# A diffusion block on one core: late modulation by PE, filter products in pairs of row halves, filter spectra from high and low parts

## The chip, the cores and the metric

The kernel runs on one core of a Trainium2 chip. The metric is the device time of one execution in microseconds; lower is better. The engines are TensorE (PE in the profile; PEld is its weight load), VectorE (DVE), ScalarE (ACT), GpSimd (POOL) and SyncE (SP). Each engine runs its own queue of instructions in order and waits for the others through semaphores. SP's queue and POOL's queue also issue the DMA transfers of this kernel.

## The reference

One layer of a transformer-like block on 1024 tokens of width 1024 with a prefix of 256 context tokens. All data are float32. What the change touches is the modulation and the filters:

```python
mod = jax.nn.silu(c) @ w_ada[i] + b_ada[i]            # (1, 6 * 1024)
mod_c = jax.nn.silu(c_ctx) @ w_ada[i] + b_ada[i]
sh1, sc1, g1, sh2, sc2, g2 = jnp.split(mod[:, None, :], N_MOD, axis=-1)
h = modulate(rmsnorm(x, norm1_g[i]), sh1, sc1)        # h * (1 + scale) + shift
q, k, v, hv, hx1, hx2, gna, ghy = jnp.split(h @ w_in[i], IN_SPLITS, axis=-1)
y_na = neighbourhood_attention(...)                   # 8 heads of 64, window 8 x 16, and all context keys
y_hy = hyena_mixer(hv, hx1, hx2, *hy_params)          # 2 long convolutions over 512 channels
x = x + g1 * gated_merge(gna, ghy, y_na, y_hy, w_na_o[i], w_hy_o[i], w_out[i])
h2 = modulate(rmsnorm(x, norm2_g[i]), sh2, sc2)
x = x + g2 * swiglu(h2, ffn_w1[i], ffn_w3[i], ffn_w2[i])   # hidden width 2816
return rmsnorm(x, final_g)

def hyena_filters(L, ...):                            # inside hyena_mixer
    hid = jnp.sin(fr * (hid @ w2 + b2))               # (1024, 64)
    h = (hid @ w3).reshape(L, 2, HY_ORDER, HY_WIDTH)  # forward and backward filter of 2 orders, 512 channels
    return h * decay[:, None, None, :]

def long_conv_bidir(u, h_fwd, h_bwd, bias):           # z = gate * this, twice
    K = jnp.fft.rfft(k2, n=2 * L, axis=0)             # k2: both filters, joined
    U = jnp.fft.rfft(u, n=2 * L, axis=1)
    y = jnp.fft.irfft(U * K[None], n=2 * L, axis=1)[:, :L]
    return y + u * bias
```

## The kernel before, in words

A tile framework schedules the program: it gives each engine a fixed order of instructions, and it allocates tiles from pools in rings. A tile's tag names its ring, and `bufs` says how many buffers the ring has; a tile that gets a buffer again waits until its former user is done. Instructions passed to `keep_in_program_order` stay in the order of the code; others the scheduler may move.

Large products are made in float32r, with each operand split into a high and a low part (`split`: ACT casts to the high part, DVE subtracts it from the source for the low part). `gemm` then adds three products, low times high, high times low and high times high (the matmuls of L194). A few products use plain float32, where the trace shows two records for each matmul (x2).

By time the stages are:

- 0 to 73 us: modulation for the first norm, the norm, and the small network that makes `hid` for the filters.
- 73 to 338 us, the filter stage. The input projection is made in 40 chunks (`proj`, tiles `in_ps` and `ctx_ps`, weights `wr` by SP, split into `wh`, `wl`). Between its pieces a side generator (`side`) makes the filters and their spectra (`filters`) and, merged with these, sums for the modulation's late parts (`ada_sums`). `_merged` interleaves generators by their yields' values against the totals that are given (`SIDE` against 39 for the projection, 97 and 39 inside the side).
- 338 to 650 us: the long convolutions (`conv`) as the side, with the projection going on.
- 650 to 805 us: neighbourhood attention with the rest of the projection.
- 805 to 950 us: the rest of attention, merged with hyena's output product (`hyena_out`, tiles `yhraw`, `hy_ps`) and with `ada_late`. This interleaving is written in the loop of `run` over `attention`.
- 950 to 1752 us: the merge, the second norm and the feed-forward network.

`filters` has four groups, one for each half of the channels and each order. A group makes 8 banks of filter products (`filt_ps`, L349), each from two float32 matmuls with 64 rows: index `j` picks rows 0 to 63 or 64 to 127 of the array. DVE multiplies a bank by `dec`, which SP loads (256 KB each, ring of 2), into `fv` (L353). Radix steps on DVE follow (`fx`, `x`, `b`), then eight DFTs of 128 points on 2 x 256 columns (`parts` makes the operand `a` on DVE and loads a matrix `matf` for two DFTs; `dft` makes three float32 matmuls, L425 to L427, into `dft_ps`). ACT copies the spectrum to `ks`, and SP stores it. The same `forward` and `dft` also serve the convolutions. The banks `f` of PSUM that `filt_ps` and `dft_ps` use are a ring of five.

`ada_sums` (L843) makes, for each of the four late parts of the modulation, the sum over 8 row blocks of `w_ada` times silu(c): SP loads `wal` (512 KB, ring of 1), and DVE does `aacc` += `wal` times a column of `cs` (L853). What is left is a sum over the 128 partitions; `aacc` is stored by POOL. `ada_late` (L857) loads the stored sums (`acc`, L868) and sums over partitions by matmuls with ones (`al_ps`, L877 to columns for the second norm's shift and scale, L890 to full tiles for the gates `g1` and `g2`).

Of the kernel before, what the change touches and what calls it, by code (L numbers as in the profile page):

```python
# [10 lines left out]
F32 = mybir.dt.float32  # L11
# [7 lines left out]
P = 128  # L19
D = 1024  # L20
# [3 lines left out]
SIDE = 460  # L24
# [18 lines left out]
def _constants():  # L43
# [15 lines left out]
    out["dft_f"], out["dft_i"] = fwd, inv  # L59

# [98 lines left out]
class Block:  # L159
# [176 lines left out]
    def filters(self, pool, psf, hid, w3):  # L336

        nc, a = self.nc, self.a
        for hf in range(2):
            for o in range(2):  # L340
                v = [pool.tile([P, 4, 2, 256], F32, tag="v8", name="fv") for _ in range(2)]
                c0 = o * 512 + hf * 256
                for n2 in range(0, 8, 2):
                    for j in range(2):
                        dec = pool.tile([P, 512], F32, tag="dec", name="dec", bufs=2)
                        nc.sync.dma_start(dec, a["decay"][hf, n2 // 2, j])
                        ps = psf.tile([P, 512], F32, tag="f", name="filt_ps")
                        for n in range(2):
                            nc.tensor.matmul(ps[:, n * 256:(n + 1) * 256],  # L349
                                             hid[64 * j:64 * j + 64, (n2 + n) * P:(n2 + n + 1) * P],  # L350
                                             w3[64 * j:64 * j + 64, c0:c0 + 256], start=True, stop=True)
                        i = n2 % 4
                        nc.vector.tensor_tensor(v[n2 // 4][:, i:i + 2, j, :], ps.rearrange("p (n c) -> p n c", n=2),  # L353
                                                dec.rearrange("p (n c) -> p n c", n=2), op=ALU.mult)
                    yield 1.3
# [11 lines left out]
                parts, spectra = self.forward(pool, psf, v[1], x)  # L367
# [10 lines left out]
    def forward(self, pool, psf, wp, wm):  # L378
# [19 lines left out]
        def parts():  # L398
# [10 lines left out]
            m = pool.tile([P, 2, 3, P], F32, tag="mat", name="matf")  # L409
            nc.sync.dma_start(m, self.a["dft_f"][ci])  # L410
            for j in range(2):
                av = pool.tile([P, 2, 256], F32, tag="a", name="a")
# [3 lines left out]
        def spectra():  # L416
            for _ in range(2):
                yield self.dft(psf, *queue.pop(0))
# [3 lines left out]
    def dft(self, psf, m, v):  # L422
# [4 lines left out]
        nc.tensor.matmul(ps[:, 256:512], m[:, 2], v[:, 0], start=False, stop=True)  # L427
        return ps
# [414 lines left out]
    def ada_sums(self, pool):  # L843

        nc, a = self.nc, self.a
        for part in range(2, 6):
            acc = pool.tile([P, D], F32, tag="aacc", name="aacc", bufs=1)
            nc.vector.memset(acc, 0.0)
            nc.sync.dma_start(acc[0:1, :], a["b_ada"][0:1, part * D:(part + 1) * D])
            for k in range(8):  # L850
                w = pool.tile([P, D], F32, tag="wal", name="wal", bufs=1)
                nc.sync.dma_start(w, a["w_ada"][k, :, part * D:(part + 1) * D])
                nc.vector.scalar_tensor_tensor(acc, w, self.cs[:, 2 * k:2 * k + 1], acc, op0=ALU.mult, op1=ALU.add)  # L853
                yield 1.2
            nc.gpsimd.dma_start(self.accd[part], acc)

    def ada_late(self, pool, psf, gates):  # L857

        nc = self.nc
        pin = self.tc.keep_in_program_order  # L860
        ones = pool.tile([P, P], F32, name="ones")
        nc.vector.memset(ones, 1.0)

        def load(part):
            accs = []
            for h in range(2):
                accs.append(pool.tile([P, 512], F32, tag="acc", name="acc", bufs=4))
                nc.sync.dma_start(accs[h], self.accd[part][:, h * 512:(h + 1) * 512])  # L868
            return accs

        queue = [(part, load(part)) for part in (3, 4)]
        yield
        ps = psf.tile([P, 512], F32, tag="f", name="al_ps")
        for n, (part, accs) in enumerate(queue):
            for k in range(8):
                at = 16 * n + 2 * k
                pin(nc.tensor.matmul(ps[:, at:at + 2], accs[k // 4][:, (k % 4) * P:(k % 4 + 1) * P], ones[:, 0:2],  # L877
                                     start=True, stop=True))
            src = ps[:, 16 * n:16 * n + 16].rearrange("p (k t) -> p k t", t=2)[:, :, 0]
            if part == 3:  # L880
                nc.vector.tensor_copy(self.mod2[:, 1, :], src)
            else:
                nc.vector.scalar_tensor_tensor(self.mod2[:, 0, :], src, 1.0, self.ng[:, 1, :],
                                               op0=ALU.add, op1=ALU.mult)
        queue = [(part, load(part)) for part in (2, 5)]
        yield
        for part, accs in queue:
            for h in range(2):
                ps = psf.tile([P, 512], F32, tag="f", name="al_ps")
                pin(nc.tensor.matmul(ps, ones, accs[h], start=True, stop=True))  # L890
# [556 lines left out]
```

## Time and profile before

| what | value |
|---|---|
| time, median of 3 runs | 1752.66 us (1752.51 to 1756.64) |
| the profiled execution's own time | 1753.88 us |
| its span, first to last instruction | 1752.0 us |
| mean granted PE clock | 0.978 |
| DMA moved | 285.36 MB, 163 GB/s |

The profile shows one execution. Busy times are of one engine over the span or over a named stretch. A row of a group gives the line, the engine, the operation with its output and inputs, the count, then busy time and mean duration, then the idle time of that engine just before these instructions with what ended it. In the timeline the columns are start, duration, engine, line, operation, count; in brackets stands the idle time before and what ended it. A PE record's duration includes its passage through the array, so that the distance between two starts is what one costs in a dense run.

### The profile page before, as it was taken

What the parts mean: (1) busy time and instruction counts of PE and PEld (TensorE: products, weight loads), DVE (VectorE), ACT (ScalarE), POOL (GpSimd) and SP (SyncE); (2) the same over time, 40 slices, a digit from 0 to 9 for tenths busy, and PEclk for the clock granted to TensorE, in tenths of its full rate; (3) what the DMA queues carried; (4) which work ended last, traced back from release to release, by engine and by line L of the source; (5) the groups of instructions that cost most, each with busy time, mean ns of one, the idle gap of its engine ahead of it and who ended that gap; (6) DMA issues with size and microseconds to landing.
All of it is one profiled execution on the core that took longest, in us unless ns stands there. A gap on an engine that the chain in (4) does not pass through costs nothing.

```text
span 1752.0 us, 22510 instructions
## 1 busy us (share of the span) xinstructions
PE 1674.1 (96%) x8128; PEld 1325.2 (76%) x8128; DVE 1227.8 (70%) x2039; ACT 663.5 (38%) x1147; POOL 143.2 (8%) x250
## 2 busy tenths in 40 slices
PE   6989898999999998999999999899999999999997
PEld 2777676777777777887777788688888888877886
DVE  5576576799887865656865867867755656479567
ACT  4611222313121213546654215733343333344555
POOL 0000110001000004011200000000100000100000
PEclk8999999999999999999999999999999999999999
DMA  8266766655464528436647424333422332295344
GB/s 352 103 220 207 224 214 201 213 162 174 145 209 148 180 73 246 129 115 192 204 157 250 158 68 144 126 120 115 150 91 91 104 107 97 102 368 186 101 120 151
DMA packets 111469, 285.36 MB, mean 163 GB/s; under 512 B 14707, under 2 KB 23543, under 8 KB 109053
## 3 DMA queue, kind: packets, MB, share of 16 engines
q1 hardware_dynamic: 91888, 221.32, 38.3%
q0 software_dynamic: 18816, 62.14, 10.4%
q8 instruction: 65, 1.06, 0.3%
q10 hardware_dynamic: 653, 0.44, 0.1%
q14 instruction: 47, 0.39, 0.1%
HBM read 213.86 MB, written 69.99 MB: 162 GB/s over the span
## 4 chain that ended last, share of the span: by engine, by line
PE 50%; issue 29%; DMA 8%; DVE 7%; ACT 3%; POOL 3%; SPq 0%; POOLq 0%; ACTq 0%; DVEq 0%
PE in_ps L194 19%; PE dx_ps L1315 5%; PE dft_ps L425 4%; PE out_ps L1089 4%; PE dz_ps L1315 3%; PE dft_ps L426 2%; PE dft_ps L427 2%; PE x_ps L1151 2%; DMA ar<-g 1%; POOL g L1263 1%; PE dy_ps L1315 1%; PE pt_ps L761 1%; PE na_ps L194 1%; PE pt_ps L775 1%; POOL g L1257 1%
## 5 line engine op out<-in xcount | busy, mean ns | idle before, releaser
L194 PE MATMUL in_ps<-hTh,wl 128*128 128x512 f32 x640 | 259.6, 406 | 5.2 <-ACT proj L596 5.2
L194 PE MATMUL in_ps<-hTl,wh 128*128 128x512 f32 x640 | 253.3, 396 | 0.0
L194 PE MATMUL in_ps<-hTh,wh 128*128 128x512 f32 x640 | 253.2, 396 | 0.0
L194 PEld LDWEIGHTS in_ps<-hTh,wl 128*128 128x128 f32 x640 | 121.8, 190 | 33.0 <-ACT proj L596 5.8
L194 PEld LDWEIGHTS in_ps<-hTh,wh 128*128 128x128 f32 x640 | 122.1, 191 | 26.6 <-issue 0.7
L194 PEld LDWEIGHTS in_ps<-hTl,wh 128*128 128x128 f32 x640 | 122.3, 191 | 25.8 <-issue 1.3
L175 DVE TENSOR_TENSOR ol<-ws,oh 128x512 fp32r<-128x512 f32 x88 | 60.5, 689 | 54.8 <-ACT oh L174 54.7
L174 ACT CAST wh<-wr 128x1024 fp32r<-128x1024 f32 x40 | 42.0, 1049 | 127.4 <-PE in_ps L194 103.5
L175 DVE TENSOR_TENSOR ol<-ar,oh 128x512 fp32r<-128x512 f32 x77 | 52.9, 688 | 49.0 <-ACT oh L174 49.0
L175 DVE TENSOR_TENSOR wl<-wr,wh 128x1024 fp32r<-128x1024 f32 x40 | 48.8, 1221 | 53.3 <-ACT wh L174 53.2
L174 ACT CAST oh<-ar 128x512 fp32r<-128x512 f32 x77 | 47.9, 622 | 84.3 <-PE dx_ps L1315 33.4
L425 PE MATMUL dft_ps<-a,matf 128*128 128x512 f32 x128 | 68.9, 621 | 10.0 <-issue 5.5
L174 ACT CAST oh<-ws 128x512 fp32r<-128x512 f32 x88 | 54.7, 622 | 53.8 <-PE x_ps L1151 23.7
L749 DVE CUSTOM_DVE_ANT_0 pe<-s_ps,bias 128x640 f32<-128x640 f32 x64 | 50.1, 819 | 30.4 <-PE s_ps L744 30.4
L853 DVE SCALAR_TENSOR_TENSOR aacc<-wal,cs,aacc 128x1024 f32<-128x1024 f32 x32 | 41.0, 1282 | 43.3 <-DMA wal<-in_w_ada 43.1
L1315 PE MATMUL dx_ps<-oh,ol 128*128 128x512 f32 x176 | 67.1, 391 | 3.6 <-DVE ol L175 3.6
L1315 PE MATMUL dx_ps<-ol,oh 128*128 128x512 f32 x176 | 68.7, 390 | 1.7 <-DVE ol L175 1.7
L750 ACT ACTIVATE pe<-pe,mx 128x640 f32<-128x640 f32 x64 | 52.6, 822 | 44.0 <-DVE mx L749 43.9
L1315 PE MATMUL dx_ps<-oh 128*128 128x512 f32 x176 | 68.5, 389 | 0.0
L175 DVE TENSOR_TENSOR ol<-wr,oh 128x512 fp32r<-128x512 f32 x70 | 48.0, 689 | 27.0 <-ACT oh L174 26.9
L174 ACT CAST oh<-wr 128x512 fp32r<-128x512 f32 x70 | 43.1, 621 | 54.6 <-PE y_ps L1151 18.2
L1091 DVE TENSOR_TENSOR x<-x,out_ps 128x512 f32<-128x512 f32 x64 | 43.5, 685 | 22.3 <-PE out_ps L1089 22.2
(392 smaller groups left out, 4236.9 us busy)
## 6 DMA issues: line engine op xcount, KB each, us to landing
wr<-in_w SPq DMA_DIRECT2D x50, 512.0 KB, 3.4
wr<-in_w_in SPq DMA_DIRECT2D x40, 512.0 KB, 4.5
ar<-g SPq DMA_DIRECT2D x77, 256.0 KB, 2.8
wal<-in_w_ada SPq DMA_DIRECT2D x32, 512.0 KB, 4.0
g<-t POOLq DMA_DIRECT2D x49, 256.0 KB, 2.8
matf<-in_dft_f SPq DMA_DIRECT2D x32, 384.0 KB, 4.9
bias<-in_rpb SPq DMA_DIRECT2D x64, 192.0 KB, 2.8
w<-in_w SPq DMA_DIRECT2D x44, 256.0 KB, 5.4
```

Source lines behind the costliest of these rows:

```text
L174: self.nc.scalar.copy(hi, src)
L175: self.nc.vector.tensor_sub(lo, src, hi.bitcast(F32))
L194: mm = nc.tensor.matmul(ps, ww[:, k * P:(k + 1) * P], xx[:, k, pos:pos + width], start=(i == 0), stop=(i == n - 1))
L425: nc.tensor.matmul(ps, m[:, 0], v.rearrange("p a b -> p (a b)"), start=True, stop=False)
L426: nc.tensor.matmul(ps[:, 0:256], m[:, 1], v[:, 1], start=False, stop=False)
L427: nc.tensor.matmul(ps[:, 256:512], m[:, 2], v[:, 0], start=False, stop=True)
L749: nc.vector.tensor_tensor_reduce(pe, ps[:, 256:896], bt, -1.0, 3e38, ALU.add, ALU.min, mx[:, 0:1])
L750: nc.scalar.activation(pe, pe, AF.Exp, bias=mx[:, 0:1], scale=-1.0, accum_out=mx[:, 1:2])
L853: nc.vector.scalar_tensor_tensor(acc, w, self.cs[:, 2 * k:2 * k + 1], acc, op0=ALU.mult, op1=ALU.add)
L1089: nc.tensor.matmul(ps, gg[x][:, tk], ww[y][:, sl], start=(i == 0), stop=(i == n - 1))
L1091: nc.vector.tensor_add(x1[:, sl], x1[:, sl], ps)
L1315: nc.tensor.matmul(ps[j], x[u][:, j * P:(j + 1) * P], w[v], start=(start and i == 0 and c == 0), stop=(stop and i == N - 1 and k == len(re ...
```

## The change

1. `ada_sums` and `ada_late` are replaced by `ada_rows`. PE multiplies the `cs` columns (32 columns) by `wal`: four float32 matmuls of 256 columns for a row block, each into another group of 32 columns of the array (L892 after), summed over eight row blocks in one bank (`ar_ps`), which holds two parts. The ring of `wal` has two buffers. DVE adds the bias row; POOL stores four short rows for each part in `modd`; four transposes turn the second norm's shift and scale into columns. The gates are later loaded from `modd` by broadcast.
2. The filter products of two banks are made in the order n, then j, kept in program order, so that neighbours use different row halves.
3. The filters' spectra use `dft_parted`: the operand is split into `ah` and `a`, the matrix `matr` holds high and low parts, and nine float32r matmuls take the place of three float32 ones. A matrix (384 KB) serves one DFT, and POOL's queue loads it. The convolutions' DFTs stay as they are.

```diff
-SIDE = 460
+SIDE = 447
...
+    out["dft_r"] = np.ascontiguousarray(np.stack([hi, fwd - hi], 3).transpose(0, 2, 1, 3, 4, 5))
...
+                    dec, ps = [], []
                     for j in range(2):
-                        dec = pool.tile([P, 512], F32, tag="dec", name="dec", bufs=2)
...
+                        dec.append(pool.tile([P, 512], F32, tag="dec", name="dec", bufs=2))
+                        nc.sync.dma_start(dec[j], a["decay"][hf, n2 // 2, j])
+                        ps.append(psf.tile([P, 512], F32, tag="f", name="filt_ps"))
+                    for n in range(2):
+                        for j in range(2):
+                            mm = nc.tensor.matmul(ps[j][:, n * 256:(n + 1) * 256],
+                                                  hid[64 * j:64 * j + 64, (n2 + n) * P:(n2 + n + 1) * P],
+                                                  w3[64 * j:64 * j + 64, c0:c0 + 256], start=True, stop=True)
+                            if n + j:
+                                self.tc.keep_in_program_order(mm)
...
-                            k = pool.tile([P, 512], F32, tag="ks", name="ks", bufs=3)
+                            k = pool.tile([P, 512], F32, tag="ks", name="ks", bufs=2)
...
+                if parted:
+                    m = pool.tile([P, 2, 3, P], F32R, tag="mat", name="matr")
+                    nc.gpsimd.dma_start(m, self.a["dft_r"][ci, j])
+                    av, ah = (pool.tile([P, 2, 256], F32R, tag=t, name=t) for t in ("a", "ah"))
+                    raw = pool.tile([P, 2, 256], F32, tag="ar", name="ar", bufs=1)
+                    nc.vector.scalar_tensor_tensor(raw, x, -g if j else g, b[:, 0], op0=ALU.mult, op1=ALU.add)
+                    self.split(ah, av, raw)
+                    queue.append((m, (ah, av)))
+                    continue
...
+    def dft_parted(self, psf, m, v):
+        ps = psf.tile([P, 512], F32, tag="f", name="dft_ps")
+        order = ((1, 0), (0, 1), (0, 0))
+        for i, (x, y) in enumerate(order):
+            nc.tensor.matmul(ps, m[:, x, 0], v[y].rearrange("p a b -> p (a b)"), start=(i == 0), stop=False)
+        for x, y in order:
+            nc.tensor.matmul(ps[:, 0:256], m[:, x, 1], v[y][:, 1], start=False, stop=False)
+        for i, (x, y) in enumerate(order):
+            nc.tensor.matmul(ps[:, 256:512], m[:, x, 2], v[y][:, 0], start=False, stop=(i == 2))
...
-    def ada_sums(self, pool):
-    def ada_late(self, pool, psf, gates):
+    def ada_rows(self, pool, psf):
...
+        for pair in ((3, 4), (2, 5)):
+            r = pool.tile([P, 512], F32, tag="arow", name="arow", bufs=1)
+            nc.gpsimd.memset(r, 0.0)
...
+                    nc.gpsimd.dma_start(r[32 * j:32 * j + 1, 256 * n:256 * n + 256], a["b_ada"][0:1, at:at + 256])
+            ps = psf.tile([P, 512], F32, tag="f", name="ar_ps")
+            for n, part in enumerate(pair):
+                for k in range(8):
+                    w = pool.tile([P, D], F32, tag="wal", name="wal", bufs=2)
+                    nc.sync.dma_start(w, a["w_ada"][k, :, part * D:(part + 1) * D])
+                    for j in range(4):
+                        nc.tensor.matmul(ps[32 * j:32 * j + 32, 256 * n:256 * n + 256], self.cs[:, 2 * k:2 * k + 32],
+                                         w[:, 256 * j:256 * j + 256], start=(k == 0), stop=(k == 7),
+                                         tile_position=(0, 32 * j))
+                    yield 0.8
+            nc.vector.tensor_add(r, ps, r)
...
+                    nc.gpsimd.dma_start(self.modd[part][0:1, 256 * j:256 * j + 256],
+                                        r[32 * j:32 * j + 1, 256 * n:256 * n + 256])
...
-                        fgen = self.filters(_Bufs(fp, t4=1, mat=2, a=2, b=4), psf, hid, w3)
-                        yield from _merged((fgen, 97), (self.ada_sums(fp), 39))
+                        fgen = self.filters(_Bufs(fp, t4=1, mat=2, a=2, ah=2, b=4), psf, hid, w3)
+                        yield from _merged((fgen, 97), (self.ada_rows(fp, psf), 26))
...
-                g1, g2 = (yp.tile([P, D], F32, name=n) for n in ("g1", "g2"))
+                nc.gpsimd.dma_start(g1, self.modd[2].broadcast_to((P, D)))
...
-                nc.sync.dma_start(self.gate2, g2)
...
-        for t, src in ((fg, a["fg"].broadcast_to((P, D))), (g2, self.gate2)):
+        for t, src in ((fg, a["fg"].broadcast_to((P, D))), (g2, self.modd[5].broadcast_to((P, D)))):
```

PE's queue at the end of a group's DFTs and the first products of the next group, before:

```order
L427 MATMUL dft_ps_1197<-a_1188,matf_1184 128x256
L349 MATMUL filt_ps_1208<-fw3_273,hid_272 128x256 x2
L349 MATMUL filt_ps_1214<-fw3_273,hid_272 128x256 x2
L349 MATMUL filt_ps_1227<-fw3_273,hid_272 128x256 x2
L349 MATMUL filt_ps_1233<-fw3_273,hid_272 128x256 x2
L349 MATMUL filt_ps_1239<-fw3_273,hid_272 128x256 x2
```

Each bank is written by two matmuls in a row, and eight banks follow one another without other work between. After, the same place, with the last rows of the group's products:

```order
L459 MATMUL dft_ps_1310<-ah_1292,matr_1289 128x256
L353 MATMUL filt_ps_1327<-fw3_272,hid_271 128x256
L353 MATMUL filt_ps_1330<-fw3_272,hid_271 128x256
...
L196 MATMUL in_ps_1399<-hTh_251,wl_1167 128x512
L353 MATMUL filt_ps_1375<-fw3_272,hid_271 128x256
L196 MATMUL in_ps_1399<-hTl_252,wh_1166 128x512
L196 MATMUL in_ps_1399<-hTh_251,wh_1166 128x512
L353 MATMUL filt_ps_1378<-fw3_272,hid_271 128x256
```

Two banks now alternate, and three matmuls of the projection stand inside the fourth pair of the group.

PE's queue at a DFT of the first group after the change, where a row block of the modulation comes between:

```order
L459 MATMUL dft_ps_1049<-ah_936,matr_933 128x256
L892 MATMUL ar_ps_843<-wal_1158,cs_240 32x256 x2
L455 MATMUL dft_ps_1062<-ah_944,matr_941 128x512
L892 MATMUL ar_ps_843<-wal_1158,cs_240 32x256 x2
L196 MATMUL in_ps_1197<-hTh_251,wh_951 128x512
...
L455 MATMUL dft_ps_1062<-a_943,matr_941 128x512
L455 MATMUL dft_ps_1062<-ah_944,matr_941 128x512
L457 MATMUL dft_ps_1062<-ah_944,matr_941 128x256
```

Matmuls of three kinds alternate there; before, three `dft_ps` matmuls stand together at such a place, with only the projection around them.

SP's queue where hyena's output begins, before (`yh` is the stored output of the convolutions, `bias` are the attention's tables):

```order
L868 DMA acc_6341<-acc3_213 128x512
L868 DMA acc_6343<-acc3_213 128x512
L868 DMA acc_6345<-acc4_214 128x512
L868 DMA acc_6347<-acc4_214 128x512
L826 DMA yhraw_6351<-yh0_100 128x512
L826 DMA yhraw_6355<-yh0_100 128x512
L868 DMA acc_6521<-acc2_212 128x512
L868 DMA acc_6523<-acc2_212 128x512
L868 DMA acc_6525<-acc5_215 128x512
L826 DMA yhraw_6359<-yh1_101 128x512
```

And after:

```order
L723 DMA kcraw_7319<-kc3_115 128x256
L858 DMA yhraw_6816<-yh0_100 128x512
L858 DMA yhraw_6820<-yh0_100 128x512
L182 DMA wfr_7086<-in_why 128x512
L763 DMA bias0_5498<-in_rpb 128x384
L763 DMA bias1_5499<-in_rpb 128x384
L858 DMA yhraw_6824<-yh1_101 128x512
L858 DMA yhraw_6828<-yh1_101 128x512
```

The eight `acc` loads are gone, and the loads of `yhraw` stand ahead of the weights `wfr` and the tables.

More of the change, by code (lines that the diff above doesn't have):

```diff
@@ L839, in hyena_out @@
                 yield
-    def ada_sums(self, pool):
+    def ada_rows(self, pool, psf):
         nc, a = self.nc, self.a
[L846 to L855, printed above, removed]
@@ L857, in ada_late @@
-    def ada_late(self, pool, psf, gates):
[L859 to L883, printed above, removed]
-                                               op0=ALU.add, op1=ALU.mult)
[L885 to L890, printed above, removed]
-                nc.scalar.copy(gates[part][:, h * 512:(h + 1) * 512], ps)
-                yield
@@ L915, in run @@
             self.hyd = [dt(f"hyo{c}", (P, T)) for c in range(8)]
-            self.accd = {j: dt(f"acc{j}", (P, D)) for j in range(2, 6)}
+            self.modd = {j: dt(f"mod{j}", (1, D)) for j in range(2, 6)}
             self.gd = [dt(f"gate{c}", (P, T)) for c in range(16)]
@@ L993, in run @@
                             next(hyena, None)
-                        elif n != 0:
-                            next(late, None)
-                    for gen in (late, hyena):
-                        for _ in gen:
-                            pass
+                    for _ in hyena:
+                        pass
                     att.close()
-                nc.sync.dma_start(self.gate2, g2)
                 psf = E3(tc.tile_pool(name="psf3", bufs=8, space=PSUM))
```

43 lines of the change are left out of this document (26 added, 17 removed).

## Prediction

> **What bounds the kernel now.** I read the page first, then the busy time by stage, then the groups and the DMA issues of the stage that the change touches, and last the timeline at the places where instructions move. The busy table and the chain of the page:
>
> ```profile
> PE 1674.1 (96%) x8128; PEld 1325.2 (76%) x8128; DVE 1227.8 (70%) x2039; ACT 663.5 (38%) x1147; POOL 143.2 (8%) x250
> PE 50%; issue 29%; DMA 8%; DVE 7%; ACT 3%; POOL 3%; SPq 0%; POOLq 0%; ACTq 0%; DVEq 0%
> ```
>
> TensorE (PE) is busy for 96% of the span, and half of the chain is PE. So a microsecond of PE work counts almost fully, and what a faster VectorE (DVE) is worth must be read stage by stage. The change touches the filter stage (73 to 338 us) and the first part of the attention beside hyena's output (805 to 836 us). Columns below: stretch, length, busy time of PE, PEld, DVE, ACT and POOL, the granted PE clock, DMA share, GB/s.
>
> ```profile
> 73.00:139.00 66.00, 60.93 (x286) 46.77 (x284) 45.62 (x58) 14.25 (x26) 3.80 (x7) 0.97 0.67 220
> 139.00:148.00 9.00, 6.76 (x35) 4.73 (x34) 5.10 (x7) 0.59 (x1) 0.00 (x0) 0.83 0.93 321
> 148.00:210.00 62.00, 57.81 (x264) 44.88 (x265) 37.98 (x44) 14.19 (x25) 5.02 (x7) 0.92 0.59 186
> 210.00:220.00 10.00, 7.35 (x42) 5.20 (x41) 5.47 (x7) 0.59 (x1) 0.00 (x0) 1.00 0.79 247
> 220.00:274.00 54.00, 53.36 (x240) 41.20 (x238) 42.54 (x55) 15.46 (x25) 6.56 (x9) 0.97 0.62 201
> 274.00:290.00 16.00, 11.33 (x49) 8.04 (x48) 6.94 (x9) 0.59 (x1) 0.00 (x0) 0.79 0.84 289
> 290.00:338.00 48.00, 48.00 (x211) 37.03 (x211) 39.99 (x55) 15.41 (x23) 5.06 (x7) 1.00 0.51 162
> ...
> 805.00:836.00 31.00, 26.23 (x216) 21.31 (x214) 22.27 (x53) 21.62 (x42) 0.56 (x1) 0.86 0.73 230
> ```
>
> In the filter stage PE idles 5.1 + 2.2 + 4.2 + 2.7 + 0.6 + 4.7 = 19.5 us. The missing clock (length times one minus the clock: 2.0 + 1.5 + 5.0 + 1.6 + 3.4) is worth 13.5 us more: 33 us lost in 265. The three short stretches are where a group of filters begins; there the DMA share is highest (0.79 to 0.93). From 805 to 836 us 4.8 us are idle and 4.3 lost to the clock. What the losses of the filter stage hang on, DVE's groups and then PE's:
>
> ```profile
> L853 DVE SCALAR_TENSOR_TENSOR aacc<-wal,cs,aacc 128x1024 f32<-128x1024 f32 x32 | 41.0, 1282 | 43.3 <-DMA wal<-in_w_ada 43.1 <-DMA aacc<-in_b_ada 0.2
> L353 DVE TENSOR_TENSOR fv<-filt_ps,dec 128x512 f32<-128x512 f32 x32 | 21.1, 683 | 10.2 <-DMA dec<-in_decay 6.7 <-PE filt_ps L349 3.5
> ...
> L848 DVE MEMSET aacc<- 128x1024 f32 x4 | 3.6, 912 | 12.7 <-DMA acc<-aacc 9.2 <-DMA matf<-in_dft_f 3.2 <-DVE hcTl L175 0.3
> ```
> ```profile
> L425 PE MATMUL dft_ps<-a,matf 128*128 128x512 f32 x64 | 36.1, 647 | 9.4 <-issue 5.5 <-DVE a L413 3.9
> L349 PE MATMUL filt_ps<-fw,hid 64*128 64x256 f32 x128 | 25.6, 414 | 10.1 <-DVE fv L353 10.1
> ```
>
> PE's 19.5 us stand in front of two kinds of matmul: the filter products, which need a free bank (the multiply by `dec` frees it), and the first DFT of a group. DVE itself stood 43 us before `aacc`, waiting for `wal`, and its queue runs in order, so part of PE's wait may be `aacc`'s doing; 6.7 us are `dec`'s own landing.
>
> **The DFTs.** A float32 DFT is three matmuls. From the first to the first of the next:
>
> ```profile
> 124.59 1.02 PE L425 MATMUL dft_ps<-a,matf 128*128 128x512 f32 x2
> ...
> 126.31 1.02 PE L425 MATMUL dft_ps<-a,matf 128*128 128x512 f32 x2
> ```
>
> That is 1.72 us. The new one is nine float32r matmuls, three of 512 columns and six of 256. The projection runs such matmuls back to back at full clock:
>
> ```profile
> 87.97 0.39 PE L194 MATMUL in_ps<-hTh,wl 128*128 128x512 f32 x1
> 88.20 0.39 PE L194 MATMUL in_ps<-hTl,wh 128*128 128x512 f32 x1
> ...
> 98.21 0.28 PE L194 MATMUL ctx_ps<-hcTl,wh 128*128 128x256 f32 x1
> 98.33 0.28 PE L194 MATMUL ctx_ps<-hcTh,wh 128*128 128x256 f32 x1
> ```
>
> So 0.23 and 0.12 us each: 3 x 0.228 + 6 x 0.119 = 1.40. 32 DFTs x 0.32 us = **10.2 us less** PE work. The parts cost a cast on ACT and a subtraction on DVE, 32 of each, like these:
>
> ```profile
> L175 DVE TENSOR_TENSOR ol<-ar,oh 128x512 fp32r<-128x512 f32 x77 | 52.9, 688 | 49.0 <-ACT oh L174 49.0
> ...
> L174 ACT CAST oh<-ar 128x512 fp32r<-128x512 f32 x77 | 47.9, 622 | 84.3 <-PE dx_ps L1315 33.4
> ```
>
> ACT gains 20 us where it has 60 busy of 265, so nothing. DVE gains 22 us and loses `aacc` with its clearing, 41.0 + 3.6: 23 us lighter. The single buffer of `ar` makes DVE wait for ACT once a DFT; the projection's work covers that except at a group's first DFT.
>
> **The filter products.** In the order n, then j, neighbours use different row halves. Of before:
>
> ```profile
> 89.11 0.39 PE L194 MATMUL in_ps<-hTh,wh 128*128 128x512 f32 x1
> 89.42 1.13 PE L349 MATMUL filt_ps<-fw,hid 64*128 64x256 f32 x4
> 90.48 0.50 PE L194 MATMUL in_ps<-hTh,wl 128*128 128x512 f32 x1
> ...
> 139.28 4.26 PE L349 MATMUL filt_ps<-fw,hid 64*128 64x256 f32 x28
> ```
>
> 28 records took 4.26 us. One after the other, at 0.215 us for 256 columns (1.72 / 8: a DFT is 2048 column passes), they would take 6.0; in perfect pairs 3.0. They overlap half already. Perfect pairs save at most 128 x (0.152 - 0.107) = 5.7 us, but behind them stands the wait for banks. I take **-2** (0 to -6).
>
> **The modulation's sums on PE.** 128 matmuls of 256 columns, four per weight row into four column groups. Before has the same form with 512 columns:
>
> ```profile
> 26.66 1.06 PE L288 MATMUL ada_ps<-wada,cs 128*32 128x512 f32 x8
> ```
>
> Eight records, that is four matmuls of two passes, took 1.06 us with their latency (0.2): 0.86, the time of one. So four with 256 columns are 0.43 us, and 32 rows 13.8. They are not in one piece: the order has about 26 visits between other matmuls. The steps around L349 at 89.42 show what a change of kind costs: 0.31 us instead of 0.23 into it and 0.34 instead of 0.23 out of it, 0.18 in all. 26 x 0.18 = 4.7. Together **+18.4** (13.8 if the changes overlap; 32 x 1.72 = 55 if the columns ran one after the other), and the four transposes +0.6.
>
> The Trainium skill ("TensorEngine Tiling (Array Packing)", Key Properties) says that the array drains when its tiling changes. The 0.18 us are what these rows show of it.
>
> **The late part.** Its matmuls and the loads ahead of hyena's go:
>
> ```profile
> L890 PE MATMUL al_ps<-acc,ones 128*128 128x512 f32 x8 | 4.5, 645 | 0.0
> L877 PE MATMUL al_ps<-ones,acc 128*128 128x2 f32 x32 | 4.1, 258 | 0.3 <-DVE mod L881 0.3
> ```
> ```profile
> 833.86 0.50 PE L194 MATMUL hy_ps<-yhh,wfl 128*128 128x512 f32 x1 [2.38 <-ACT yhh L174]
> ```
> ```profile
> 810.74 0.91 SPq L826 DMA_DIRECT2D yhraw<-yh  x2
> 814.55 2.52 SPq L868 DMA_DIRECT2D acc<-acc  x3
> ```
>
> 4.5 + 4.1 us of PE go, at a clock of 0.86. Hyena's inputs `yhraw` move up past the eight `acc` loads on SP, so the 2.4 us wait at 833.86 may go. But the attention's steps here wait for softmax, and PE with less to fill in may idle instead. **-9** (-4, half of the matmuls; -13, matmuls and 4.4 of the 9.1 us lost). The gates' broadcasts (POOL, SP) replace the `acc` and `gate2` transfers and land long before their use: 0.
>
> **The waits of the filter stage.** This is the largest uncertainty. What feeds it:
>
> ```profile
> wal<-in_w_ada SPq DMA_DIRECT2D x32, 512.0 KB, 4.0
> dec<-in_decay SPq DMA_DIRECT2D x32, 256.0 KB, 4.2
> ...
> matf<-in_dft_f SPq DMA_DIRECT2D x16, 384.0 KB, 4.9
> acc<-aacc POOLq DMA_DIRECT2D x4, 512.0 KB, 5.6
> ```
> ```profile
> 134.09 0.54 POOL L855 DMA_DIRECT2D acc<-aacc  x1 [17.07 <-DVE x L408]
> ```
>
> A matrix of 384 KB now serves one DFT instead of two, through the same two buffers, on POOL's queue; POOL's stores in this queue (`qk`, `kc`, `vtok`) come between. By the rows a matrix takes 4.9 us to land; where the order puts DFTs densest, at some 7 places, the DFT that needs the freed buffer follows after 3.5 to 4.2 us of PE work (their matmuls by the pitches above): with POOL's 0.5 for the issue 1.2 to 1.9 us each, 11 us of waits (2 if it lands in 4, as a `wal` does; 25 if it takes 6.3, above the 5.6 of the POOL row). PE now frees `wal` (two buffers, 4.0 us, against 3.0 to 3.5 us of work between rows in the densest places, again some 7): 6 (2 to 14). SP's queue stands behind each `wal` that waits, with `dec` and the spectra's stores. The first DFT of each group keeps 6, `dec` 3, half clock 5. That makes 31 in place of 33: **-2** (-15 to +20, from these bounds).
>
> What a wait does beyond its length:
>
> ```profile
> 218.33 1.13 PE L349 MATMUL filt_ps<-fw,hid 64*128 64x256 f32 x4 [2.65 <-DVE fv L353]
> ...
> 219.96 0.63 PE L194 MATMUL in_ps<-hTh,wl 128*128 128x512 f32 x1
> ```
>
> After a wait of 2.65 us the same matmul takes 0.63 instead of 0.39 us. The Trainium skill ("TensorE: Matmul & The Clock Gate", Why this matters for your kernels) would have only gaps above some 3.4 us cost clock; here the shorter one did, so I let waits of 2 us count for clock as well.
>
> **The sum.** -10.2 - 2 + 18.4 + 0.6 - 9 - 2 = -4.2 us. The profiled execution took 1753.9 us (span 1752.0 and 1.9 around it), 1.2 above the median 1752.66: 1752.7 - 4.2 = 1748.5, said as **1748 us**. Less than 0.3% (5.3 us) can't be told from no change.
>
> **The rivals.**
>
> *The waits go with `aacc`.* For it: 43.1 us of DVE's waiting stood before `aacc`, in the queue that frees banks and makes `a`. Against it: 6.7 us of `fv`'s wait is `dec`'s own, and the DMA share there stays. If 14 of the 31 us that I let stand go too: 1734 (1726 to 1741).
>
> The Trainium skill ("DMA: Bandwidth & Descriptors", Anatomy of one DMA, SWDGE (gpsimd) path) fits 2.0 us plus bytes at 436 GB/s for such a transfer: an estimate of 2.9 us for a matrix, by which the matrix waits vanish and the sum is about -15. No load of this size from POOL's queue stands in before.
>
> *The matrices stop PE.* The other side, by one mechanism: two buffers with one DFT each. Each microsecond that a matrix takes beyond 4.9 adds some 10 us (7 places, and the half clock behind). It decides from about 5.8 us, where the sum is +5; at 6.3 it is +10: 1762 (1754 to 1775). For it: the DMA share of 0.79 to 0.93 where groups begin, and 16 more matrices of 384 KB. Against: 0.6 elsewhere.
>
> *The columns don't overlap* beside single visits, at 1.7 us a row instead of 0.43: +40, 1780 and more. The row at 26.66 speaks against it.
>
> *The late part brings nothing*, because softmax sets the pace there: 1757 (1752 to 1760).
>
> **How the numbers follow.** The sum as worked (1742 to 1754): 0.45, of which 0.20 is faster by over 0.3% and 0.25 within. Waits go: 0.22, faster. Matrices stop PE: 0.20, 0.06 within and 0.14 slower. Columns one after the other: 0.05, slower. Late part brings nothing: 0.08, 0.06 within and 0.02 slower. Faster 0.42, within 0.3% 0.37, slower 0.21. The range 1731 to 1766 takes the first case and that of the late part whole, 0.14 of the 0.22 where waits go and 0.13 of the 0.20 where matrices stop PE, 0.80 in all; the likeliest's own is 1742 to 1754.
>
> **What would show it.** After: nine float32r matmuls per DFT in 1.4 us; four `ar_ps` matmuls of a visit in about 0.6 us; `matr`'s median landing near 4.9; the first `dft_ps` matmuls' idle time near 11 us by `matr`, not by DVE; the stretch before conv ending within 5 us of 338 + 5 (the sum without the late part); hyena's first matmuls without the wait for `yhh`. The prediction is wrong if the loss of the filter stage leaves 20 to 45 us, or if a visit costs over 0.9 us.

## Result and profile after

The changed kernel takes 1774.51 us (median; 1770.77 to 1774.82) against 1752.59 of the kernel before: a ratio of 1.0122, with a 95% interval of 1.0100 to 1.0143. It is slower by some 22 us, above the predicted range. The profiled execution has a span of 1772.7 us.

Busy table and chain of the page, to be read against those of before:

```profile
PE 1674.5 (94%) x8444; PEld 1325.3 (75%) x8444; DVE 1208.2 (68%) x2036; ACT 678.4 (38%) x1175; POOL 175.8 (10%) x313
PE 58%; DVE 5%; issue 5%; DMA 5%; ACT 2%; POOL 0%; SPq 0%; DVEq 0%; POOLq 0%; ACTq 0%
```

PE is as busy as before (1674.5 against 1674.1 us), and the span is 20.7 us longer. So in sum the loss is idle PE. The filter stage by stretches (the columns of the prediction; the stage now ends later, so a last stretch is added):

```profile
73.00:139.00 66.00, 58.29 (x363) 42.85 (x362) 41.40 (x59) 18.61 (x33) 11.93 (x23) 1.00 0.74 237
139.00:148.00 9.00, 7.37 (x38) 5.79 (x40) 1.55 (x3) 1.17 (x2) 1.05 (x2) 0.81 1.00 310
148.00:210.00 62.00, 53.63 (x289) 40.84 (x288) 34.39 (x46) 14.82 (x26) 10.01 (x18) 0.92 0.59 186
210.00:220.00 10.00, 10.00 (x50) 8.12 (x50) 1.61 (x3) 1.17 (x2) 0.54 (x1) 1.00 0.62 186
220.00:274.00 54.00, 49.13 (x311) 37.09 (x310) 35.51 (x50) 16.40 (x29) 12.08 (x20) 1.00 0.61 187
274.00:290.00 16.00, 11.04 (x51) 8.05 (x52) 2.41 (x4) 3.54 (x8) 3.41 (x6) 0.75 0.83 275
290.00:338.00 48.00, 46.68 (x256) 35.23 (x253) 37.36 (x55) 12.21 (x20) 4.93 (x8) 0.98 0.56 173
338.00:360.00 22.00, 18.84 (x103) 14.83 (x102) 9.50 (x15) 8.42 (x14) 7.13 (x13) 1.00 0.68 199
```

PE idles 32.0 us in these 287 us; the kernel before idles 20.5 in the same ones. In the three short stretches the idle time fell from 9.6 to 6.6 us, in the others (73 to 139, 148 to 210, 220 to 274, 290 to 338 us) it rose from 9.9 to 22.3. The missing clock, by the same rows, is 11.6 us, against 13.5 before. What PE waits for, in us, times, longest (73 to 365 us):

```profile
PE dft_ps L455 <- DMA matr<-in_dft_r: 20.7, 12, 3.9
PE ar_ps L892 <- DMA wal<-in_w_ada: 5.1, 5, 2.4
PE filt_ps L353 <- DVE fv L360: 3.0, 1, 3.0
PE ar_ps L892 <- DMA wr<-in_w_in: 1.9, 1, 1.9
PE dft_ps L455 <- ACT ah L176: 0.4, 1, 0.4
```

The waits for `fv` fell from 10.1 to 3.0 us, and those for `a` and issue are gone. In their place stand the matrices with 20.7 us and the weight rows with 7.0. One cycle of it, in PE's timeline, POOL's, and PE's again:

```profile
119.67 0.28 PE L459 MATMUL dft_ps<-ah,matr 128*128 128x256 f32 x1
```
```profile
120.25 0.53 POOL L424 DMA_DIRECT2D matr<-in_dft_r  x1 [3.31 <-PE dft_ps L459]
```
```profile
123.15 0.40 PE L196 MATMUL in_ps<-hTh,wh 128*128 128x512 f32 x1
125.85 0.47 PE L455 MATMUL dft_ps<-ah,matr 128*128 128x512 f32 x1 [2.30 <-DMA matr<-in_dft_r]
126.16 0.40 PE L196 MATMUL in_ps<-hTh,wl 128*128 128x512 f32 x1
126.39 0.39 PE L196 MATMUL in_ps<-hTl,wh 128*128 128x512 f32 x1
```

The DFT that holds the buffer ends at 119.95 (119.67 + 0.28). POOL has waited for it 3.31 us and starts the next matrix at 120.25. The DFT that needs it starts 5.60 us later, at 125.85, with PE idle for the last 2.30. At the 12 waits the time from POOL's issue to the DFT is 4.2 to 7.3 us, 5.6 on average, and the landing alone, counted from the start of the issue, 5.5. POOL issued within 0.8 us of the buffer's release at 11 of them. At one it issued 4.3 us late, since a store ahead in its queue (`vctok`) waited for ACT; that wait of 1.9 us hangs on the queue, not on the ring alone. The transfers' medians in the stage (SP's and POOL's queue):

```profile
wal<-in_w_ada SPq DMA_DIRECT2D x32, 512.0 KB, 4.9
matr<-in_dft_r POOLq DMA_DIRECT2D x32, 384.0 KB, 4.7
```

For a balance I give each instant from 73 us to the last matmul of the projection to the PE instruction that then runs (from its start to the next start or its own end), with the rest as idle. Smaller kinds are left out, so the rows shown don't add up to the last one (us):

| | before | after | dft_only | rows_only | no_parted | hi_ring4 | mat4 | mat4_half |
|---|---|---|---|---|---|---|---|---|
| filters' DFTs | 58.9 | 51.7 | 49.0 | 55.6 | 55.7 | 50.3 | 54.2 | 51.3 |
| filter products | 24.7 | 24.1 | 26.3 | 23.7 | 21.7 | 22.6 | 27.4 | 26.1 |
| `ar_ps` | 0 | 17.9 | 0 | 17.5 | 17.5 | 18.5 | 18.3 | 30.1 |
| `in_ps` (1824 each) | 435.2 | 437.7 | 436.6 | 432.6 | 430.5 | 431.9 | 438.4 | 437.3 |
| idle | 26.1 | 39.9 | 39.5 | 17.1 | 20.8 | 25.9 | 37.5 | 24.9 |
| whole stretch | 731.6 | 758.6 | 738.1 | 737.6 | 734.8 | 738.3 | 764.5 | 759.2 |

Each column is one execution. It lies up to 4.4 us from its kernel's median (`mat4_half` 4.4 and `rows_only` 3.8 above, `no_parted` 3.3 below), so differences of a few us between columns need not be the kernels'.

Up to there the change loses 27.0 us. From there to hyena's last matmul it gains 3.8 (145.0 to 141.2), and behind that 2.5 (802.4 to 799.9), against a span 20.7 longer.

### The profile page after: what moved, and what is told of

Same layout as the page of the kernel before. It is cut to its first block, busy times and chain, and to the rows that moved or that the text cites. A ratio compares the mean times of both kernels' runs of the same rounds, so it can differ in the third digit from the quotient of the medians.

```text
span 1772.7 us, 23235 instructions
## 1 busy us (share of the span) xinstructions
PE 1674.5 (94%) x8444; PEld 1325.3 (75%) x8444; DVE 1208.2 (68%) x2036; ACT 678.4 (38%) x1175; POOL 175.8 (10%) x313
## 4 chain that ended last, share of the span: by engine, by line
PE 58%; DVE 5%; issue 5%; DMA 5%; ACT 2%; POOL 0%; SPq 0%; DVEq 0%; POOLq 0%; ACTq 0%
PE x_ps L1160 13%; PE in_ps L196 12%; PE z_ps L1160 7%; PE dx_ps L1324 6%; PE out_ps L1098 3%; PE dz_ps L1324 3%; PE y_ps L1160 2%; PE dft_ps L444 2%; PE na_ps L196 1%; PE dy_ps L1324 1%; PE dft_ps L445 1%; PE dft_ps L446 1%; PE pt_ps L793 1%; DMA yhraw<-yh 1%; DMA kraw<-qk 1%
## 5 line engine op out<-in xcount | busy, mean ns | idle before, releaser
L176 ACT CAST oh<-ws 128x512 fp32r<-128x512 f32 x88 | 54.7, 622 | 51.7 <-PE x_ps L1160 21.7
L360 DVE TENSOR_TENSOR fv<-filt_ps,dec 128x512 f32<-128x512 f32 x32 | 21.5, 689 | 56.1 <-PE filt_ps L353 25.8
L793 PE MATMUL pt_ps<-ident,pe 128*128 128x128 f32 x320 | 44.1, 286 | 10.9 <-ACT yrow L814 7.7
```

Source lines behind the costliest of these rows:

```text
L176: self.nc.scalar.copy(hi, src)
L360: nc.vector.tensor_tensor(v[n2 // 4][:, i:i + 2, j, :], ps[j].rearrange("p (n c) -> p n c", n=2), dec[j].rearrange("p (n c) -> p n c", n=2 ...
L793: pin(nc.tensor.transpose(pt[:, at:at + P], pe[:, c * P:(c + 1) * P], self.ident))
```

## Experiments

Theory A: the matrices' ring, with one DFT for each of two buffers, makes PE wait, and that is the loss. Theory B: the modulation's rows on PE are the loss. Ratios are to the kernel before, run on the same chip.

**One part alone.** `dft_only` is before with this part, `rows_only` is before with `ada_rows` (and its `SIDE` of 447), and `no_parted` is the changed kernel without this part:

```diff
-    parts, spectra = self.forward(pool, psf, v[1], x)
+    parts, spectra = self.forward(pool, psf, v[1], x, True)
```

> Only the filters' spectra by nine float32r products; the modulation's sums and the filter products stay as before. Theory A (the two-buffer ring of matrices, one DFT each, makes PE wait): the DFTs' own work falls by 6 to 7 us as in the changed kernel, the first dft_ps matmuls wait some 20 us for matr, so 1760 to 1768. Theory B (the sums on PE are what costs): no harm without them, 1742 to 1749.

> Only the modulation's sums by PE; filter products and spectra as before. Theory A: PE gains 18 us of ar_ps work and some 3 us at the projection's neighbours, DVE's old waits (fv, a, issue: 19.5 us before) mostly go, the late part gives 4: 1750 to 1758. Theory B: the visits and the waits for wal cost more than they free, 1764 to 1775.

> The changed kernel with the filters' spectra as before (float32, matf for two DFTs, by SP). Theory A: the 20.7 us of waits for matr go and 6.5 us of DFT work come back: 1750 to 1760. Theory B: within 5 us of the changed kernel, 1769 to 1780.

Measured: `dft_only` 1757.48 us, 1.0034 (1.0015 to 1.0054). `rows_only` 1749.03, 0.9990 (0.9973 to 1.0007). `no_parted` 1749.31, 0.9989 (0.9973 to 1.0006). Theory B falls: the rows and the pairs together cost nothing. Taking the spectra out of the changed kernel gains 23 us by the ratios (25 by the medians, which come from different chips), while on their own they cost 6. That is less than theory A's 8 to 16 and more than theory B's nothing, so `dft_only` lies in neither range; the other two lie a microsecond below theory A's. PE's waits in `dft_only`, then in `no_parted`:

```profile
PE dft_ps L450 <- DMA matr<-in_dft_r: 14.2, 13, 3.0
PE filt_ps L351 <- DVE fv L355: 9.1, 4, 4.9
PE dft_ps L450 <- ACT ah L176: 5.1, 3, 2.3
```
```profile
PE ar_ps L865 <- DMA wal<-in_w_ada: 5.7, 6, 2.3
PE filt_ps L351 <- DVE fv L358: 4.8, 3, 2.6
```

The waits for matrices are there as soon as the new spectra are, with or without the rows. In `dft_only`, where DVE is still late, less of them shows: 14.2 instead of 20.7 us. `rows_only` and `no_parted` differ in the pairing alone and have the same time; in the balance the products take 2.0 us less of PE and idle time is 3.7 longer, both within the spread of single executions.

**The matrix loads.** Half the load, with four buffers and with two:

```diff
-    m = pool.tile([P, 2, 3, P], F32R, tag="mat", name="matr")
-    nc.gpsimd.dma_start(m, self.a["dft_r"][ci, j])
+    m = pool.tile([P, 1, 3, P], F32R, tag="mat", name="matr")
+    nc.gpsimd.dma_start(m, self.a["dft_r"][ci, j][:, 0:1])
```

> The changed kernel, but of each matrix only the high part is loaded (192 KB instead of 384) and used in the place of the low part too, with four buffers in the same space. It leaves out the low parts of the matrices; the matmuls are as many as in the changed kernel. Theory A: the waits for matr fall from 20.7 us to under 4, 1750 to 1758. Theory B: 1768 or more, since the rows on PE stay.

> As hi_ring4 (only the high parts of the matrices are loaded, 192 KB, and used twice), but with two buffers as in the changed kernel. If the size of the load and its landing are what matters, the waits for matr are near those of hi_ring4 (under 6 us) and the time 1750 to 1756. If the look-ahead matters (a load starts only when the DFT before last ends, whatever its size), the waits stay above 12 us and the time is 1762 to 1775.

> The changed kernel with three buffers for the matrices; the space comes from the ring of x3, two buffers to one, which DVE alone writes and reads. Full matrices of 384 KB. Theory A (look-ahead): a load starts one DFT earlier, the waits for matr fall from 20.7 to 4 to 8 us, 1757 to 1764. If the landing under load from other transfers is what matters, the waits stay above 12 us and the time above 1766.

`hi_ring4` took 1752.11 us, 1.0005 (0.9988 to 1.0022); `hi_ring2` 1762.05, 1.0061 (1.0045 to 1.0076); `mat3` 1765.07, 1.0067 (1.0042 to 1.0091). PE's longest waits in `hi_ring4`, `hi_ring2` and `mat3`:

```profile
PE dft_ps L455 <- ACT ah L176: 6.7, 3, 3.2
PE ar_ps L892 <- DMA wal<-in_w_ada: 4.6, 5, 2.2
```
```profile
PE dft_ps L455 <- DMA matr<-in_dft_r: 11.6, 8, 3.6
```
```profile
PE dft_ps L455 <- DMA matr<-in_dft_r: 10.0, 4, 3.0
PE ar_ps L892 <- DMA wal<-in_w_ada: 6.1, 5, 2.4
```

With both, the waits for matrices are gone and so are 20 us by the ratios. Half the size alone gives 11 (its median landing is 3.7 us), two more buffers on top 10. One more buffer at full size gives 10. So a shorter landing and more look-ahead each give back about half; which share is whose depends on the order, since four buffers at full size, below, leave no wait for matrices either. I had set them up as an either-or. `hi_ring2` lies at the near edge of the range for look-ahead and its 11.6 us are between the two expectations; the 1765.07 and 10.0 us of `mat3` lie between its two as well.

**Four full buffers in the changed kernel** need space. In `mat4` it came from `ks`, in `mat4_half` from `wal`; `ks1` and `ks3` change `ks` alone, apart from the one buffer for `x3` that all four have:

```diff
-    fgen = self.filters(_Bufs(fp, t4=1, mat=2, a=2, ah=2, b=4), psf, hid, w3)
+    fgen = self.filters(_Bufs(fp, t4=1, t2=1, mat=4, a=2, ah=2, b=4), psf, hid, w3)
...
-    k = pool.tile([P, 512], F32, tag="ks", name="ks", bufs=2)
+    k = pool.tile([P, 512], F32, tag="ks", name="ks", bufs=1)
```

> Four buffers for the matrices, as much look-ahead as the matrices for two DFTs gave before; ks and x3 have one buffer each, and the small bias row uses the buffer of ar. Theory A: waits for matr under 3 us, 1750 to 1757, unless the single ks makes ACT late for the banks (then 1757 to 1765).

> The changed kernel with one buffer for ks (x3 has one). It separates mat4's slowness: if the single ks costs 15 to 20 us there (the waits for ah), here it adds to the waits for matr in part, 1780 to 1792. If it costs nothing, 1771 to 1778, and mat4's loss has another cause.

> The changed kernel with three buffers for ks as in the kernel before (x3 has one). If the cut of ks from three to two holds ACT at the spectra's stores and so makes the split (ah) and the banks late, this gives back 4 us or more: under 1770. If not, 1771 to 1778.

> The changed kernel with four buffers for the full matrices and two for ks, as the change has them; the space comes from wal, which is loaded in halves of 256 KB through three buffers, from x3's ring and the bias row. Theory A: no waits for matr and few for ah, as in hi_ring4, 1750 to 1757. If the four full matrices make ACT and DVE late also without the single ks, 1765 or more.

`mat4` took 1776.38 us, 1.0133 (1.0098 to 1.0167): above both of its ranges and no better than the change. `ks1` took 1768.66, 1.0104 (1.0088 to 1.0120), `ks3` 1771.23, 1.0120 (1.0095 to 1.0144), `mat4_half` 1768.38, 1.0109 (1.0086 to 1.0131). PE's first wait in `mat4` and ACT's; then PE's in `mat4_half`, and its group of `ar_ps`:

```profile
PE dft_ps L455 <- ACT ah L176: 15.7, 9, 4.4
```
```profile
ACT ks L379 <- DMA spec<-ks: 67.8, 22, 8.2
```
```profile
PE ar_ps L894 <- DMA wal<-in_w_ada: 11.8, 7, 4.6
PE filt_ps L353 <- DVE fv L360: 2.1, 1, 2.1
```
```profile
L894 PE MATMUL ar_ps<-wal,cs 128*32 128x256 f32 x256 | 33.2, 407 | 11.9 <-DMA wal<-in_w_ada 11.8
```

In `mat4` no wait for matrices is left, but with one `ks` ACT stands before the spectra's stores, and the cast for `ah` stands behind it in ACT's queue. With two `ks` buffers, in `mat4_half`, the waits for `ah` are 0.9 us. My expectation for `ks1` missed, its time being below both ranges: the single buffer costs nothing in the changed kernel. ACT stands before the stores there too (57.8 us), but PE stands for matrices anyway (17.3 us). I read this as two limits one behind the other; `mat4_half` changes `wal` as well, so no run shows the effect of `ks` with four matrices by itself. That the cut of `ks` from three to two cost something is not shown: `ks3` has the change's time. The time of `mat4_half` lies in the range of its second case, but not by that case's mechanism. It lost its gain elsewhere: the half rows come in 45 visits instead of 26, 30 of them of a single half row, and the rows take 30.1 us of PE instead of 17.9, with 11.8 us of waits for `wal`.

**Four buffers without the rows.** `dft_mat4` is `dft_only` with the rings of `mat4`, but with two buffers for `ks`:

> As dft_only (only the spectra changed, sums on DVE as before), with four buffers for the matrices; x3 has one buffer and the bias row uses the buffer of ar. Theory A: the 14.2 us of waits for matr in dft_only fall under 3, DVE's waits (fv 9.1, ah 5.1) stay: 1741 to 1750. If the waits only move to DVE and ACT, as they did with four buffers in the changed kernel, 1753 to 1760.

1749.56 us, 0.9982 (0.9964 to 0.9999), 9 less than `dft_only` by the ratios. PE's waits:

```profile
PE dft_ps L450 <- ACT ah L176: 8.0, 4, 2.6
PE filt_ps L351 <- DVE fv L355: 7.4, 4, 3.2
PE dft_ps L450 <- DVE a L177: 4.8, 2, 4.0
```

The waits for matrices are gone here too, this time with complete matrices. The new spectra are then worth 3 us, barely clear of noise, and not the 10 of their matmuls. PE now waits more for the results of the split, 12.8 us for the cast (`ah`) and the subtraction (`a`) together, against 5.1 in `dft_only`.

**The old waits.** To see what `aacc` in DVE's queue cost, without work for PE:

```diff
-    nc.vector.scalar_tensor_tensor(acc, w, self.cs[:, 2 * k:2 * k + 1], acc, op0=ALU.mult, op1=ALU.add)
+    nc.gpsimd.tensor_scalar(w, w, self.cs[:, 2 * k:2 * k + 1], None, op0=ALU.mult)
+    nc.gpsimd.tensor_tensor(acc, w, acc, op=ALU.add)
```

> The kernel before with the late sums made by POOL (a multiplication by the column of cs and an addition, and the clearing of aacc) in place of DVE's 32 scalar_tensor_tensor. PE gets no work for it. It tests the rival that the old waits hang on aacc in DVE's queue: if so, PE's waits for fv and a (14.0 us, with 5.5 of issue) fall under 6 us and the time is 1736 to 1744. If they are dec's own landing and the shared transfers, 1748 to 1756. If POOL is slower than the loads allow, the sums run late into conv and wal holds up SP's queue: above 1760.

1865.43 us, 1.0661 (1.0627 to 1.0694). It doesn't test the rival, since POOL is too slow (its two groups; then DVE's multiply by `dec`):

```profile
L853 POOL TENSOR_SCALAR wal<-wal,cs 128x1024 f32<-128x1024 f32 x32 | 104.4, 3263 | 125.7 <-DMA wal<-in_w_ada 125.7
L854 POOL TENSOR_TENSOR aacc<-wal,aacc 128x1024 f32<-128x1024 f32 x32 | 79.6, 2489 | 4.7 <-DMA aacc<-in_b_ada 2.5
```
```profile
L353 DVE TENSOR_TENSOR fv<-filt_ps,dec 128x512 f32<-128x512 f32 x32 | 21.7, 688 | 118.2 <-DMA dec<-in_decay 98.4 <-PE filt_ps L349 19.8
```

A row takes 5.8 us instead of DVE's 1.3, `wal` has one buffer, and `dec` stands behind it in SP's queue: 98 us of waits. `rows_only` bears on the rival, since PE replaces DVE there: its waits for `fv` are 3.3 us instead of 10.1, and those for `a` (4.6) and issue (5.5) are gone. It is no clean test. PE has 17.5 us more work of its own there, in which DVE can catch up, so that `aacc` in DVE's queue made the old waits is argued, not shown.

**A version faster than both.** From `no_parted`: two row blocks for each visit of PE, kept together, with four `wal` buffers:

```diff
+    ws = [pool.tile([P, D], F32, tag="wal", name="wal", bufs=4) for _ in range(2)]
...
+                            if i + j:
+                                self.tc.keep_in_program_order(mm)
-                    yield 0.8
+                    yield 1.6
```

> As no_parted (float32 spectra, rows by PE), but two row blocks of the modulation for each visit, with four buffers for wal; ks has two buffers and x3 one. Theory: 17 visits in place of 25 save about 8 x 0.18 = 1.4 us, and the 5.7 us of waits for wal go: 1740 to 1746. If the waits for wal only turn into others (banks, dec, behind wal in SP's queue), 1747 to 1752.

> As bunch, with three buffers for dec (the bias row takes a buffer of x3's ring). If the remaining waits of PE for fv (4.1 us) are dec's landing, they fall under 2 us: 1741 to 1746. If not, as bunch, 1745 to 1750.

`bunch` took 1747.28 us, 0.9976 (0.9957 to 0.9995). `bunch_dec3` took 1745.46, 0.9968 (0.9952 to 0.9984): 7 us below the kernel before on the same chip (1752.73), and 27 below the change by the ratios. PE's waits in `bunch_dec3`:

```profile
PE dft_ps L430 <- issue: 5.0, 3, 3.8
PE filt_ps L351 <- DVE fv L358: 3.8, 2, 2.7
PE ar_ps L868 <- DMA wal<-in_w_ada: 2.3, 2, 1.2
```

The waits for `wal` are 2.3 us instead of the 5.7 of `no_parted`, and in `bunch` they are gone; waits for other things came in their place, 5.0 us of issue here. So `bunch` came out at the lower edge of its second range. Its 19 visits instead of 26 saved no PE work either: the rows take 18.3 us (18.0 in `bunch_dec3`) against 17.5. The third `dec` left the waits for `fv` as they were (4.1 and 3.8 us). Both kernels are slightly faster than before (0.2 and 0.3%), but the intervals overlap with that of `no_parted`, so that the larger visits and the third `dec` gain anything over it is not shown.

## Why the prediction was wrong

The step that failed is "the waits of the filter stage", priced at -2 (-15 to +20). In the balance it came out at +16.3: 13.8 us more idle time, and 2.5 more in `in_ps` for the same matmuls. That lies within the step's own bounds, so what was wrong is its size and sign, and the weight given to one mechanism of it. Of the 25 us between the forecast sum (-4.2) and the span (+20.7) it makes 18. The late part makes 5, the DFTs 3 and the pairs 1; the rows and what lies behind hyena take some 3 off.

- Its mechanism for the loss was named, as the rival "the matrices stop PE", and that is what happened. Its condition was wrong: I let it decide by the landing, from 5.8 us, and the median landing is 4.7. A single wait is of the size that I took, 1.7 us on average (1.2 to 1.9 in the prediction); there are 12 of them and not 7. 20.7 us in place of 11. I also added POOL's 0.5 for the issue to a landing that is counted from its start; what lies between a buffer's release and the issue is 0.3 at most of the places. The other estimate, 2.9 us for a matrix, is below every landing measured (3.4 to 9.4).
- The rows' waits were 7.0 where I took 6. The old waits went further than I let them, to 3.4 us in place of 9 for `dec` and the first DFT, as in the rival "the waits go with `aacc`". So both rivals on waits came true at once, and the second was larger.
- Half clock is not what made `in_ps` longer: the clock lost between 73 us and the projection's end is 17.1 us before and 13.7 after. What rose is the number of `in_ps` matmuls with other work or idle time right behind them, from 71 to 117.
- The DFTs gained 7.2 us instead of 10.2. Undisturbed a DFT takes what was worked out, here at full clock from one to the next:

```profile
132.24 0.40 PE L455 MATMUL dft_ps<-ah,matr 128*128 128x512 f32 x1
...
133.65 0.39 PE L455 MATMUL dft_ps<-ah,matr 128*128 128x512 f32 x1
```

  1.41 us, against 1.40 worked out. On average it is 1.62 (51.7 / 32) and even in `hi_ring4` 1.57, with half clock and other matmuls between. The old one, too, was 1.84 on average (58.9 / 32) and not 1.72.
- The rows on PE: 17.9 us measured, 18.4 predicted, and 0.5 for the transposes. This term held, and so did the overlap of the four column groups and the 26 visits. A visit of one row block and one of two:

```profile
89.44 0.64 PE L892 MATMUL ar_ps<-wal,cs 128*32 128x256 f32 x8
105.17 1.07 PE L892 MATMUL ar_ps<-wal,cs 128*32 128x256 f32 x16
```

  The second block adds 0.43 us, as worked out; a visit costs some 0.14 beyond that (0.18 in the prediction).
- The pairs: -0.6 us of PE time, with -2 predicted; -2.0 between `rows_only` and `no_parted`, and no gain in time.
- The late part: -3.8 us, with -9 predicted and -4 as its bound. Kernels without it take 137.6 to 142.4 us from the projection's end to hyena's, those with it 143.0 to 147.0. PE's work there fell by the 9.0 us that were forecast, and the wait before the second pair of `hy_ps` chunks is gone, but PE's idle time in this stretch rose from 7.8 to 13.0 us. That it would was written down as a doubt and left out of the price.
- The range's upper end, 1766, was below the measured time because I gave the case of the matrices 0.20 and so cut its upper half (to 1775) off.
- Of the signs that I named, the DFT's 1.4 us, the visit's 0.6 and the landing near 4.9 came as said. The waits by `matr` (20.7 us, not 11) and the stage's end (the filters' last DFT ends at 354.9 us, before at 336.0) did not. The loss of the filter stage, 32.0 us idle and 11.6 of clock, stayed within 20 to 45: that band was too wide to tell the miss.

The spectra cost 23 us on top of the other parts and 6 alone. The balance says where. Put into the kernel before, the rows cut idle time by 9.0 us (26.1 to 17.1), the DFTs by 3.3 and `in_ps` by 2.6, which with 5.0 of the late part makes up for their 17.5. Put on top of the new spectra they cut none of these: against `dft_only` idle time is 0.4 longer (39.5 to 39.9), the DFTs 2.7 and `in_ps` 1.1. So the rows fill idle time in the one kernel and not in the other. Why stays open. That DVE's delays and the matrices' waits overlap in `dft_only`, so that removing the first only shows the second, is argued from the two tables of waits, not shown by a run of its own.

## What to carry to other kernels

When a change makes a tile serve half as much work, its ring may need twice as many buffers: here 12 of 32 uses waited for their transfer, and none did with four buffers. Compare the time between uses with issue to use at the densest places, not with the median landing, and count these places. A limit costs time only where no other hides it: the single `ks` went with waits for `ah` of 15.7 us in `mat4` and of 3.5 in `ks1`. An engine's freed time is worth what its waiters gain: in `rows_only` 41 us less on DVE and 18 more on PE came out even.

## What the runs showed of the hardware

- Two column groups cost PE as much as four. In `mat4_half` a visit of half a row, two matmuls of 256 columns, takes as long as one of four matmuls after the change (0.64 us, row at 89.44):

```profile
99.46 0.63 PE L894 MATMUL ar_ps<-wal,cs 128*32 128x256 f32 x4
```

- Waits of similar length cost clock in one place and not in another: after the 2.30 us before 125.85 the projection's matmuls still start 0.23 us apart (126.16 and 126.39), while of before a wait of 2.65 us was followed by half clock. My reading of the rows of before as a rule for 2 us was too simple. The granted clock in the records changes only at steps of 3.41 us (within 3 ns in all 16 traces). Stretches between such steps, of before around the wait that ends at 218.33 and of after around the one that ends at 125.85 (length, busy time of PE, PEld, DVE, ACT and POOL, clock, DMA share, GB/s):

```profile
216.54:219.95 3.41, 1.62 (x6) 1.15 (x7) 2.34 (x3) 0.00 (x0) 0.00 (x0) 1.00 0.62 193
219.95:223.36 3.41, 3.41 (x9) 2.67 (x8) 1.63 (x2) 0.00 (x0) 0.00 (x0) 0.50 0.58 223
```
```profile
121.57:124.99 3.42, 1.98 (x12) 1.37 (x10) 3.04 (x6) 1.40 (x3) 0.53 (x1) 1.00 0.87 224
124.99:128.40 3.41, 2.55 (x14) 2.27 (x15) 1.39 (x2) 0.83 (x2) 0.15 (x1) 1.00 0.72 189
```

  In before 1.79 us of idle time fall into one stretch, and the next runs at half clock. After, the wait is split into 1.44 and 0.86 us, and the clock stays. From 60 us on, none of the 7610 stretches of the 16 traces that kept the full clock had more than 1.90 us of idle time, and 114 of the 137 that lost it did. The Trainium skill ("TensorE: Matmul & The Clock Gate", "What's actually happening" in Part 1) has the clock follow activity in windows of some 3.4 us that run on freely. The traces agree, with steps of 3.41 us. The 3.4 us of the prediction stand in that part too, while the section that it names says some 3; by the rows above, 1.79 us of idle time in one stretch were enough.
- While POOL computed in `pool_sums`, DVE's `a`, which reads two tensors of SBUF, took 960 ns on average instead of 686; the multiply of `filt_ps` (PSUM) by `dec` stayed at 688 (row above). Not every operation on two tensors of SBUF slowed: the split's `wl` kept its 1219 ns. Why is not shown.

```profile
L413 DVE SCALAR_TENSOR_TENSOR a<-x,b 128x512 f32<-128x512 f32 x24 | 22.7, 960 | 10.8 <-PE dft_ps L427 10.6
```
